# One ring of small buffers for residual rows and weight sums, the second SwiGLU product opened inside the first, and the residual added late

## The chip, the cores and the metric

The kernel runs on one core of a Trainium2 chip. The time is the device time of one execution in microseconds (us), lower is better; the figure of a kernel is the median of its timed runs. Every array is float32.

## The reference, cut to what matters

One layer of an encoder with 1024 frames (S) of 1024 channels (D): a mixer of two recurrent branches with a residual, then a SwiGLU with a residual, then a last RMS norm. The mixer is untouched here. The SwiGLU has 2816 hidden channels.

```python
def swiglu(xn, w_ffn_in, w_ffn_out):
    gate, up = _split(xn @ w_ffn_in, (D_FF, D_FF))
    return (jax.nn.silu(gate) * up) @ w_ffn_out
...
        h = h + hybrid_mixer(rms_norm(h, norm1_g[l]), ...)
        h = h + swiglu(rms_norm(h, norm2_g[l]), w_ffn_in[l], w_ffn_out[l])
    return rms_norm(h, norm_f)
```

## The kernel before

**Precision.** A float32 operand is kept as a high part (rounded to the matmul's type) and a low part. `split` makes them: ScalarE casts the high part (L84), VectorE subtracts it from the source (L85). A product is then three matmuls: high by high, high by low, low by high.

**Loads.** `add` puts a load into a plan, `load_next` issues the next one (L96, on SP's queue), `split_next` splits the oldest loaded tile and issues the next load. The raw tiles are two buffers, `w_raw`, used in turn (`act_raw` uses the same two).

**Order.** Each engine runs its own instructions in a fixed order, which the tile scheduler writes when the program is built; an instruction that waits holds up all that stand behind it on its engine. A tile named with a `tag` and `bufs` is one of a ring of so many buffers; the next user of a buffer waits for the last reader of the former. Pools that are opened after others are closed lie on the same memory and wait in the same manner.

**p5: the mixer's last projection and the second norm.** `hres[c]`, eight tiles of 128 rows (chunks c = 0 to 7), hold the residual. For each chunk `out_proj` (L147 with `mm`) adds the projection to it, `norm2_rows` norms it into `xr` and stores the row to `h_dram`, and `norm2_turn` transposes it on TensorE (L201), copies the result on ScalarE to `xb` (L858) and forms the differences of Winograd's form of Strassen's product on VectorE and GpSimd (L862 to L865). From these `block` splits seven operands of 4 x 512 columns: `b11`, `b21`, `t1`, `t2`, `b22`, `t3`, `t4`. The second half (`t1` to `t4`, `b22`) needs chunk 7.

**ffn_in: the first product.** A unit u (22 of them) is 128 gate and 128 up channels. It is seven products p of 12 matmuls of 128x128 by 128x512 (`product`, L809), in the order of the list `seq`; the weight of product (u, p) is a block of the raw weight or one of four sums (`unit_sums`, four GpSimd instructions L797 to L800, into `s1` to `s4`), split into a tile `wc` (`weight`; three buffers are in the pool `wearly`, five in the pool of ffn_in). After some products `after` evacuates the PSUM bank: `e1` (L934), `sg` (silu, L937), `u2`, `e5`, `u3` and so on; after product 4 the activation row `act` is stored to `act_dram` (L956). Weights are prepared four products ahead (`LEAD`). Units 0 and 1 begin inside p5, with products (0,1) and (1,1); their evacuations and sums come after p5.

**ffn_out: the second product.** The 22 chunks of hidden channels are cut into pieces of (4, 4, 4, 4, 4, 2). For each piece its weights and activation rows are loaded and split into `slot` tiles; then for each chunk c of rows and each half of columns `mm_tok` does 3 matmuls for each hidden chunk (L147 with `aux`), and VectorE adds the bank to `hres[c]` (L1046), which was loaded again from `h_dram` (L1027, tiles `hr`). In the last piece ScalarE squares and sums the row (L1048) into `o`, of two buffers `o7`; VectorE forms the factor and the output (L1061, for the last half row ScalarE at L1059), and two stores of a half row each go out (L1063).

Of the kernel before, what the change touches and what calls it, by code (L numbers as in the profile page):

```python
# [9 lines left out]
F32 = mybir.dt.float32  # L10
# [3 lines left out]
ALU = mybir.AluOpType  # L14
# [18 lines left out]
def hybrid_block_kernel(  # L33
# [780 lines left out]
    hres = [h_pool.tile([P, D], F32, name=f"h{c}") for c in range(NC)]  # L814
# [4 lines left out]
    def weight(u, p, pool=None):  # L819
# [4 lines left out]
        wready[u, p] = t  # L824

    with phase("p5", "right") as pp:
# [66 lines left out]
        for c in range(4, NC):  # L893
# [8 lines left out]
            if c == 6:  # L902
                unit_load(1)
                weight_a = {1: raws[0][0][:, 0:4], 2: raws[0][0][:, 4:8]}
                sums[0] = weight_a
                weight(0, 1)
                weight(0, 2)
        turn_late()
        sums[1] = {1: raws[1][0][:, 0:4]}
        weight(1, 1)  # L910
        banks = {}
# [4 lines left out]
        for name, src, i, j in (("t1", xb[0][0], 0, 0), ("t2", t2, 0, 0), ("b22", xb[1][1], 1, 1),  # L916
                                ("t3", xb[1][0], 1, 1), ("t4", xb[0][1], 0, 1)):
            block(name, src, i, j)
    h_stack.close()


    with phase("ffn_in", "right") as pp:
        def tmp(tag, bufs):
            t = pp.tile([P, 512], F32, name=tag, tag=tag, bufs=bufs)
            return t

        part = {}

        def after(u, p):
            b1, b2, b3 = banks[u, 1], banks.get((u, 6)), banks.get((u, 5))  # L930
            d = part.setdefault(u, {})
            if p == 1:
                d["e1"] = tmp("e1", 2)
                nc.scalar.copy(out=d["e1"], in_=b1)  # L934
            elif p == 2:
                d["sg"] = tmp("sg", 2)
                nc.scalar.activation(out=d["sg"], in_=b1, func=AF.Silu)  # L937
            elif p == 6:
                d["u2"] = tmp("u2", 2)
                nc.vector.tensor_tensor(out=d["u2"], in0=b2, in1=d["e1"], op=ALU.add)  # L940
            elif p == 5:
# [25 lines left out]
        def prepare(i):  # L967
            if i >= len(seq) or seq[i] in wready:
                return
# [126 lines left out]
```

## Time and profile before

| | us |
|---|---|
| median of three timed runs | 2128.44 (2128.12 to 2130.18) |
| the profiled execution's own time | 2135.46 |
| its span | 2133.8 |
| TensorE busy in the span | 2032.1 |
| VectorE, ScalarE, GpSimd busy | 1234.2, 839.4, 446.3 |

The profiled execution is one execution with the profiler on, and it took 7.0 us longer than the median. Its span runs from the first to the last recorded instruction. The first SwiGLU product lies between 1408 and 1852 us of the span, the second between 1852 and the end. The mean granted clock of TensorE is 0.981 of full speed.

### The profile page before, as it was taken

The page shows a single profiled execution, that of the slowest core. Times are in us where ns is not written, and L with a number is a line of the kernel's source. Part 1 is how long each engine was busy: PE and PEld are TensorE (multiplying, and loading weights), DVE is VectorE, ACT ScalarE, POOL GpSimd, SP SyncE. Part 2 cuts the span into 40 slices and gives each one's busy share as a digit, 9 for nine tenths or more (in the row PEclk, how much of TensorE's full clock was granted, in tenths as well). Part 3 has the DMA queues.
Part 4 walks back from the last instruction along what each step waited for, and adds up shares of the span by engine and source line. Part 5 has one row for each costly group of instructions (what it writes and reads, how often), then busy time and mean ns, then how long its engine had stood idle before and what let it go on. Part 6 is the DMA issues. An engine that isn't in the chain of part 4 may idle for free.

```text
span 2133.8 us, 23957 instructions
## 1 busy us (share of the span) xinstructions
PE 2032.1 (95%) x9206; PEld 1659.8 (78%) x9206; DVE 1234.2 (58%) x2178; ACT 839.4 (39%) x1156; POOL 446.3 (21%) x318
## 2 busy tenths in 40 slices
PE   6999999999999998999999999979999999789996
PEld 4778888777787786788888888858888888678885
DVE  6677667778768779634431215567455555344436
ACT  5886744544544544421131113443333333222202
POOL 3100004324324325200100110025333333000000
PEclk9999999999999999999999999989999999999998
DMA  3222231322321321322141114322222223343302
GB/s 131 62 70 61 81 104 41 95 87 65 89 76 59 114 75 50 109 89 89 50 128 50 50 50 162 105 77 76 85 79 90 88 63 96 137 150 117 108 33 79
DMA packets 178806, 182.28 MB, mean 85 GB/s; under 512 B 9404, under 2 KB 145028, under 8 KB 178692
## 3 DMA queue, kind: packets, MB, share of 16 engines
q1 hardware_dynamic: 178692, 180.76, 27.0%
q8 instruction: 72, 1.18, 0.2%
q14 instruction: 42, 0.34, 0.1%
HBM read 148.10 MB, written 32.64 MB: 85 GB/s over the span
## 4 chain that ended last, share of the span: by engine, by line
PE 76%; DVE 12%; DMA 6%; issue 3%; ACT 2%; POOL 0%; SPq 0%; DVEq 0%; ACTq 0%; POOLq 0%
PE mm L136 34%; PE mm L809 19%; PE aux L147 11%; PE mm L147 8%; DVE ed L546 2%; DMA ed<-acs_dram 2%; DMA w_raw<-in_w_in_dram 2%; PE aux L592 1%; DVE rs_t L158 1%; DVE ed L574 1%; DMA act_raw<-act_dram 1%; PE aux L425 1%; DVE w_lo L85 1%; DMA y_dram<-xd 1%; DVE rs_r L160 1%
## 5 line engine op out<-in xcount | busy, mean ns | idle before, releaser
L809 PE MATMUL mm<-slot,wc 128*128 128x512 f32 x1848 | 426.9, 393 | 14.5 <-ACT e L934 13.9
L809 PEld LDWEIGHTS mm<-slot,wc 128*128 128x128 f32 x1848 | 348.6, 189 | 91.4 <-ACT e L934 14.2
L136 PE MATMUL mm<-xn_lo,w_hi 128*128 128x512 f32 x896 | 355.0, 396 | 0.6 <-DVE xn_lo L206 0.6
L136 PE MATMUL mm<-xn_hi,w_hi 128*128 128x512 f32 x896 | 355.2, 397 | 0.0
L136 PE MATMUL mm<-xn_hi,w_lo 128*128 128x512 f32 x896 | 354.4, 396 | 0.0
L147 PE MATMUL aux<-slot,slot 128*128 128x512 f32 (+1 forms) x1062 | 246.9, 395 | 16.5 <-ACT slot L84 11.2
L147 PEld LDWEIGHTS aux<-slot,slot 128*128 128x128 f32 x1062 | 202.1, 191 | 61.4 <-ACT slot L84 12.5
L136 PEld LDWEIGHTS mm<-xn_lo,w_hi 128*128 128x128 f32 x896 | 170.5, 190 | 37.9 <-DVE xn_lo L206 1.1
L136 PEld LDWEIGHTS mm<-xn_hi,w_lo 128*128 128x128 f32 x896 | 170.4, 190 | 37.3
L136 PEld LDWEIGHTS mm<-xn_hi,w_hi 128*128 128x128 f32 x896 | 170.1, 190 | 36.5
L85 DVE TENSOR_TENSOR w_lo<-w_raw,w_hi 128x1024 fp32r<-128x1024 f32 x80 | 106.7, 1334 | 139.1 <-ACT w_hi L84 139.0
L147 PE MATMUL mm<-wz,xn_hi 128*128 128x512 f32 x512 | 161.3, 395 | 0.0
L84 ACT CAST w_hi<-w_raw 128x1024 fp32r<-128x1024 f32 x80 | 83.6, 1045 | 178.1 <-PE mm L136 157.4
L1046 DVE TENSOR_TENSOR hr<-aux,hr 128x512 f32<-128x512 f32 (+1 forms) x97 | 65.3, 683 | 97.8 <-PE aux L147 97.7
L147 PEld LDWEIGHTS mm<-wz,xn_hi 128*128 128x128 f32 x512 | 94.5, 188 | 18.5
L147 PE MATMUL mm<-wz,xn_lo 128*128 128x512 f32 x256 | 101.1, 395 | 0.0
L84 ACT CAST slot<-w_raw 128x1024 fp32r<-128x1024 f32 x34 | 35.5, 1051 | 166.2 <-PE aux L147 80.3
L84 ACT CAST wc<-s 128x512 fp32r<-128x512 f32 x88 | 54.4, 620 | 113.1 <-PE mm L809 108.5
L85 DVE TENSOR_TENSOR wc<-s,wc 128x512 fp32r<-128x512 f32 x88 | 74.2, 845 | 36.2 <-ACT wc L84 34.9
L546 DVE TENSOR_SCALAR ed<-ed,acs_t 128x128 f32<-128x128 f32 x256 | 80.8, 381 | 22.5 <-DMA ed<-acs_dram 22.3
L147 PE MATMUL mm<-slot,slot 128*128 128x512 f32 x384 | 89.2, 391 | 0.0
L136 PE MATMUL mm<-v_even,w_hi 128*128 128x512 f32 x256 | 84.7, 405 | 0.0
(270 smaller groups left out, 3231.1 us busy)
## 6 DMA issues: line engine op xcount, KB each, us to landing
w_raw<-in_w_in_dram SPq DMA_DIRECT2D x72, 512.0 KB, 3.9
ed<-acs_dram SPq DMA_DIRECT2D x32, 512.0 KB, 4.3
w_raw<-in_w_branch_dram SPq DMA_DIRECT2D x24, 512.0 KB, 3.4
w_raw<-in_w_ffn_in_dram SPq DMA_DIRECT2D x22, 512.0 KB, 3.9
raw_pair<-in_w_ffn_in_dram SPq DMA_DIRECT2D x22, 512.0 KB, 5.3
act_dram<-act SPq DMA_DIRECT2D x22, 512.0 KB, 2.9
w_raw<-in_w_ffn_out_dram SPq DMA_DIRECT2D x22, 512.0 KB, 3.6
act_raw<-act_dram SPq DMA_DIRECT2D x22, 512.0 KB, 3.9
```

The costliest lines, as they stand in the source:

```text
L84: nc.scalar.copy(out=hi, in_=src)
L85: nc.vector.tensor_tensor(out=lo, in0=src, in1=f32(hi), op=ALU.subtract)
L136: nc.tensor.matmul(ps[:m, :], ww[:, k, :], xx(p, k, h), start=(k == 0 and i == 0), stop=(k == nk - 1 and i == 2))
L147: nc.tensor.matmul(ps, xx(p, k), ww(q, k), start=(k == 0 and i == 0), stop=(k == nk - 1 and i == 2))
L158: nc.vector.tensor_tensor(out=t, in0=r, in1=r, op=ALU.mult)
L160: nc.vector.scalar_tensor_tensor(out=r, in0=t, scalar=1.5, in1=r, op0=ALU.add, op1=ALU.mult)
L425: nc.tensor.matmul(pg, w[:, j, :], uu[:, hs], start=(q == 0), stop=(q == 2))
L546: nc.vector.tensor_scalar(out=ed[:, h, :], in0=ed[:, h, :], scalar1=acs_t[:, c, h0 + h:h0 + h + 1], scalar2=0.0, op0=ALU.subtract, op1=ALU ...
L574: nc.vector.tensor_tensor(out=ed, in0=ed, in1=sc.unsqueeze(1).broadcast_to([P, HG, P]), op=ALU.mult)
L592: nc.tensor.matmul(pd[:, h * 64:(h + 1) * 64], ed[:, h, :], xdt[:, h, :], start=True, stop=True)
L809: nc.tensor.matmul(ps, w[:, p, k, :], x[q][:, k, :], start=(start and k == 0 and i == 0), stop=(k == 3 and i == 2), skip_group_check=True)
L1046: nc.vector.tensor_tensor(out=hres[c][:, ns], in0=po, in1=hres[c][:, ns], op=ALU.add)
```

## The change

Four things change.

A ring `hbuf` of eight buffers of 128x1024 float32 holds the residual rows of p5, and after them the sums of a unit (in two pairs, `s12` and `s34`), `e1` with `sg`, `u2` with `u3`, and `e5`. It stays open until the end of ffn_in.

The sums of units 0 and 1 are made inside p5, at chunks 5 and 6. Their products (0,1), (1,1) and now also (0,2) are issued there with their evacuations.

The second product's plan is made before ffn_in, with pieces of (2, 4, 4, 4, 4, 4). In the last unit, 21, two loads are issued after product 6 and one item is split after each of the products 5, 2, 7 and 3: the whole first piece.

The rows are no longer loaded ahead of the second product. ScalarE copies the first piece's result into `hres[c]` (L1056 after), and in the third piece (`f0 == 6`) the row is loaded from `h_dram` into `hl` (L1049) and added by GpSimd (L1050). The PSUM banks of the second product come in turn from the rings `aux` (three) and `mm` (four).

```diff
+    def hbuf(name, shape):
+        t = h_pool.tile(shape, F32, name=name, tag="hbuf", bufs=8)
+        return t
+
+    hres = [hbuf(f"h{c}", [P, D]) for c in range(NC)]
...
-    def unit_sums(u, pool):
+    def unit_sums(u):
...
-        s1, s2, s3, s4 = (pool.tile([P, 4, P], F32, name=f"s{i}", tag="wsum", bufs=4) for i in range(1, 5))
+        (s1, s2), (s3, s4) = ([t[:, 0], t[:, 1]] for t in (hbuf("s12", [P, 2, 4, P]), hbuf("s34", [P, 2, 4, P])))
...
+    def pair(u, name):
+        t = hbuf(name, [P, 2, 512])
+        return t[:, 0], t[:, 1]
...
         if p == 1:
-            d["e1"] = tmp("e1", 2)
+            d["e1"], d["sg"] = pair(u, "e1_sg")
...
-            if c == 6:
+            if c == 5:
                 unit_load(1)
+                unit_sums(0)
                 weight(0, 1)
                 weight(0, 2)
+            if c == 6:
+                unit_sums(1)
+                weight(1, 1)
         turn_late()
-        for u, p in ((0, 1), (1, 1)):
-            banks[u, 1] = bank("mm")
-            product(banks[u, 1], wready.pop((u, p)), xc[XOF[p]], True)
+        opened(0, 1)
+        opened(1, 1)
         turn_late()
+        block("t1", xb[0][0], 0, 0)
+        opened(0, 2)
+        block("t2", t2, 0, 0)
...
-        seq = [(0, 2), (0, 5), (0, 6), (0, 3), (0, 7), (1, 6), (0, 4), (1, 5), (1, 2), (1, 7), (1, 3), (2, 1), (1, 4)]
+        seq = [(1, 2), (0, 5), (0, 6), (0, 3), (0, 7), (1, 6), (0, 4), (1, 5), (1, 7), (1, 3), (2, 1), (1, 4)]
...
+            opened(u, p)
+            if u == NFT - 1:
+                if p == 6:
+                    load_next()
+                    load_next()
+                elif p in (5, 2, 7, 3):
+                    split_next()
...
-        for nk in (4, 4, 4, 4, 4, 2):
+    for nk in (2, 4, 4, 4, 4, 4):
...
-        for c in range(NC):
-            nc.sync.dma_start(out=hres[c], in_=h_dram[c * P:(c + 1) * P, :])
...
+                if f0 == 6:
+                    hl = pp.tile([P, D], F32, name="hl", tag="hl", bufs=2)
+                    nc.sync.dma_start(out=hl, in_=h_dram[c * P:(c + 1) * P, :])
+                    nc.gpsimd.tensor_tensor(out=hres[c], in0=hres[c], in1=hl, op=ALU.add)
...
-                    po = bank()[:, :b - a]
+                    po = bank("mm" if c % 2 else "aux")[:, :b - a]
...
+                    if not f0:
+                        nc.scalar.copy(out=hres[c][:, ns], in_=po)
+                        continue
```

The diff says little of the order on the engines, so three places are shown. The first is TensorE's order where row chunk 7 is transposed (`xr_10479` before, `xr_10494` after, is chunk 7's normed row; `slot_10316` and `slot_10317` are `b11`, `slot_10363` and `slot_10364` are `b21`, `slot_10571` and `slot_10572` are `t1`). Before:

```order
L809 MATMUL mm<-slot_10317,wc 128x512
L809 MATMUL mm<-slot_10316,wc 128x512
L201 MATMUL aux<-ident,xr_10479 128x128 x8
L809 MATMUL mm<-slot_10363,wc 128x512
L809 MATMUL mm<-slot_10364,wc 128x512
```

After:

```order
L809 MATMUL mm<-slot_10363,wc 128x512 x2
L809 MATMUL mm<-slot_10364,wc 128x512
L809 MATMUL mm<-slot_10363,wc 128x512
L201 MATMUL aux<-ident,xr_10494 128x128 x8
L809 MATMUL mm<-slot_10363,wc 128x512
L809 MATMUL mm<-slot_10364,wc 128x512
L809 MATMUL mm<-slot_10571,wc 128x512
L809 MATMUL mm<-slot_10572,wc 128x512
```

Before, the transposes stand right behind product (1,1) and ahead of (0,2); after, they stand behind (0,2), and (1,2) is the first product behind them, woven with the first two matmuls of (0,5).

The second place is ScalarE's order there, from chunk 6's last copies to the casts of the last blocks. Before:

```order
L858 COPY xb_10395<-aux 128x4x128
L84 CAST wc<-w_raw 128x512
L858 COPY xb_10396<-aux 128x4x128
L858 COPY xb_10395<-aux 128x4x128
L858 COPY xb_10396<-aux 128x4x128
L84 CAST slot_10567<-xb_10396 128x1024 x2
L84 CAST slot_10555<-xb_10041 128x1024 x2
L84 CAST slot_10573<-xb_10395 128x1024 x2
L84 CAST slot_10561<-t_9799 128x1024 x2
L934 COPY e_10590<-mm 128x512
L934 COPY e_10592<-mm 128x512
L84 CAST wc<-s_10594 128x512
```

After (`s_10443` is a sum of unit 1):

```order
L905 COPY xb_10410<-aux 128x4x128
L842 COPY e_sg<-mm 128x512
L905 COPY xb_10411<-aux 128x4x128
L84 CAST wc<-s_10443 128x512
L842 COPY e_sg<-mm 128x512
L84 CAST wc<-w_raw 128x512
L844 ACT_TABLE_LOAD
L844 ACTIVATE e_sg<-mm 128x512
L84 CAST wc<-s_10443 128x512
L905 COPY xb_10410<-aux 128x4x128
L905 COPY xb_10411<-aux 128x4x128
L84 CAST slot_10596<-xb_10411 128x1024 x2
L84 CAST slot_10571<-xb_10041 128x1024 x2
```

The first evacuations, two casts of unit 1's sums and the silu with its table load have moved ahead of chunk 7's copies (the last two `xb` rows), and the `e1` copies no longer stand behind the casts of `t`.

The third place is SP's queue of DMA issues around the last unit. Before:

```order
L956 DMA act_dram<-act 128x1024 x2
L96 DMA w_raw<-in_w_ffn_out_dram 128x2x512
L96 DMA act_raw<-act_dram 128x1024
L956 DMA act_dram<-act 128x1024
L1027 DMA hr_13577<-h_dram 128x1024
L1027 DMA hr_13578<-h_dram 128x1024
L1027 DMA hr_13579<-h_dram 128x1024
L96 DMA w_raw<-in_w_ffn_out_dram 128x2x512
L1027 DMA hr_13580<-h_dram 128x1024
L96 DMA act_raw<-act_dram 128x1024
L1027 DMA hr_13581<-h_dram 128x1024
L1027 DMA hr_13582<-h_dram 128x1024
```

After:

```order
L96 DMA act_raw<-act_dram 128x1024
L96 DMA w_raw<-in_w_ffn_out_dram 128x2x512
L862 DMA act_dram<-act 128x1024 x2
L96 DMA act_raw<-act_dram 128x1024
L96 DMA w_raw<-in_w_ffn_out_dram 128x2x512
L96 DMA act_raw<-act_dram 128x1024
L96 DMA w_raw<-in_w_ffn_out_dram 128x2x512
L1036 DMA g_bc_13526<-in_norm_f_dram 128x1024
L1049 DMA hl<-h_dram 128x1024 x2
L96 DMA act_raw<-act_dram 128x1024
L862 DMA act_dram<-act 128x1024
L96 DMA w_raw<-in_w_ffn_out_dram 128x2x512
```

Before, the loads of the rows `hr` stand between the first loads of the second product. After, those eight are gone from there; the first item's loads stand ahead of two stores of `act`, and the store of unit 21's `act` stands behind three more activation rows, two weights, `g_bc` and two loads of `hl`.

## Rows read from the trace of the kernel before

**Rows 1.** The page's chain that ended last: share of the span by engine.

```profile
PE 76%; DVE 12%; DMA 6%; issue 3%; ACT 2%; POOL 0%; SPq 0%; DVEq 0%; ACTq 0%; POOLq 0%
```

**Rows 2.** The page's groups: name and shapes xcount | busy, mean ns | idle before, releaser.

```profile
L809 PE MATMUL mm<-slot,wc 128*128 128x512 f32 x1848 | 426.9, 393 | 14.5 <-ACT e L934 13.9
...
L147 PE MATMUL aux<-slot,slot 128*128 128x512 f32 (+1 forms) x1062 | 246.9, 395 | 16.5 <-ACT slot L84 11.2
...
L1046 DVE TENSOR_TENSOR hr<-aux,hr 128x512 f32<-128x512 f32 (+1 forms) x97 | 65.3, 683 | 97.8 <-PE aux L147 97.7
```

**Rows 3.** Table of stretches: length, busy time of each engine, PEclk, DMA share, GB/s.

```profile
1420.00:1436.00 16.00, 4.66 (x11) 3.71 (x12) 13.41 (x11) 8.08 (x11) 6.76 (x5) 0.50 0.00 0
1550.00:1840.00 290.00, 290.00 (x1269) 237.95 (x1268) 148.38 (x195) 96.54 (x164) 99.22 (x71) 1.00 0.25 80
1858.00:1870.00 12.00, 5.58 (x13) 4.10 (x14) 2.45 (x2) 2.09 (x2) 0.00 (x0) 0.50 1.01 400
1890.00:2080.00 190.00, 190.00 (x840) 157.34 (x839) 86.26 (x103) 33.26 (x32) 0.00 (x0) 1.00 0.28 89
```

**Rows 4.** Timeline of TensorE, gap 1: start, length, line, tiles [idle before <-releaser].

```profile
1416.33 1.06 PE L201 MATMUL aux<-ident,xr 128*128 128x128 f32 x8 [1.18 <-DVE xr L847]
1431.34 11.98 PE L809 MATMUL mm<-slot,wc 128*128 128x512 f32 x40 [13.95 <-ACT e L934]
1443.85 6.46 PE L809 MATMUL mm<-slot,wc 128*128 128x512 f32 x27 [0.53 <-DVE wc L85]
```

**Rows 5.** Timeline of VectorE, gap 1.

```profile
1410.26 0.69 DVE L862 TENSOR_TENSOR xb<-xb,xb 128x512 f32<-128x512 f32 x1
...
1417.61 1.45 DVE L862 TENSOR_TENSOR xb<-xb,xb 128x512 f32<-128x512 f32 x1 [0.23 <-ACT xb L858]
...
1420.37 7.97 DVE L85 TENSOR_TENSOR slot<-xb,slot 128x1024 fp32r<-128x1024 f32 x6
1428.26 2.34 DVE L85 TENSOR_TENSOR slot<-t,slot 128x1024 fp32r<-128x1024 f32 x2
```

**Rows 6.** Timeline of ScalarE and GpSimd, gap 1.

```profile
1416.86 1.65 POOL L865 TENSOR_TENSOR xb<-xb,t 128x512 f32<-128x512 f32 x1 [3.36 <-DVE t L863]
...
1430.70 1.07 ACT L934 COPY e<-mm 128x512 f32<-128x512 f32 x2 [4.93 <-DVE slot L85]
1430.74 1.29 POOL L797 TENSOR_TENSOR s<-w_raw 128x512 f32<-128x512 f32 x1 [9.16 <-issue]
...
1438.01 1.28 ACT L937 ACT_TABLE_LOAD   x1
```

**Rows 7.** Timeline of TensorE, gap 2.

```profile
1852.31 0.63 PE L147 MATMUL aux<-slot,slot 128*128 128x512 f32 x2
...
1864.42 7.91 PE L147 MATMUL aux<-slot,slot 128*128 128x512 f32 x21 [8.81 <-ACT slot L84]
...
1875.99 4.13 PE L147 MATMUL aux<-slot,slot 128*128 128x512 f32 x11 [0.76 <-DVE slot L85]
1882.49 77.88 PE L147 MATMUL aux<-slot,slot 128*128 128x512 f32 x335 [2.37 <-DVE hr L1046]
```

**Rows 8.** Timeline of ScalarE, gap 2.

```profile
1863.32 1.04 ACT L84 CAST slot<-w_raw 128x1024 fp32r<-128x1024 f32 x1 [10.32 <-DMA w_raw<-in_w_ffn_out_dram]
...
1885.58 1.04 ACT L84 CAST slot<-w_raw 128x1024 fp32r<-128x1024 f32 x1 [2.76 <-DMA w_raw<-in_w_ffn_out_dram]
...
1898.19 1.05 ACT L84 CAST slot<-w_raw 128x1024 fp32r<-128x1024 f32 x1 [1.64 <-DMA w_raw<-in_w_ffn_out_dram]
```

**Rows 9.** DMA issues from 1835 to 1900: xcount, KB each, median us to landing.

```profile
hr<-h_dram SPq DMA_DIRECT2D x8, 512.0 KB, 9.1
w_raw<-in_w_ffn_out_dram SPq DMA_DIRECT2D x7, 512.0 KB, 3.7
```

**Rows 10.** Timeline of the last 74 us: TensorE's last row, ScalarE's last square.

```profile
2059.71 56.01 PE L147 MATMUL aux<-slot,slot 128*128 128x512 f32 x252
...
2126.58 0.40 ACT L1048 ACTIVATE o<-hr 128x256 f32<-128x256 f32 x1
```

More of the change, by code (lines that the diff above doesn't have):

```diff
@@ L912, in hybrid_block_kernel @@
[L912 to L914 removed]
+        opened(0, 1)
+        opened(1, 1)
         turn_late()
[L916 to L917 removed]
+        block("t1", xb[0][0], 0, 0)
+        opened(0, 2)
+        block("t2", t2, 0, 0)
+        for name, src, i, j in (("b22", xb[1][1], 1, 1), ("t3", xb[1][0], 1, 1), ("t4", xb[0][1], 0, 1)):
@@ new lines, in hybrid_block_kernel, with add_act, then, act_raw @@
+    acts, pieces, f0 = {}, [], 0
+    def add_act(f):
+        def then(raw):
+            acts[f] = slot(1)
+            split(acts[f][:, 0, :], acts[f][:, 1, :], raw)
+        def act_raw():
+            t = stream.tile([P, S], F32, name="act_raw", tag="w_raw", bufs=2)
+            return t
+        add(act_dram[f * P:(f + 1) * P, :], then, act_raw)
+    def add_wf(n, q, f0, wf):
+        def then(raw):
+            if q == 0:
+                wf[n] += [quad(slot(0)), quad(slot(0))]
+            split(wf[n][0][:, 2 * q:2 * q + 2, :], wf[n][1][:, 2 * q:2 * q + 2, :], raw)
+        add(w_cols(w_ffn_out, n * 512, 512, (f0 + 2 * q) * P, 2), then)
@@ L961, in hybrid_block_kernel @@
+    for nk in (2, 4, 4, 4, 4, 4):
+        wf = [[], []]
+        pieces.append((f0, nk, wf))
+        for n in range(2):
+            for q in range(nk // 2):
+                add_act(f0 + n * (nk // 2) + q)
+                add_wf(n, q, f0, wf)
+        f0 += nk
+    with phase("ffn_in", "right") as pp:
+        seq = [(1, 2), (0, 5), (0, 6), (0, 3), (0, 7), (1, 6), (0, 4), (1, 5), (1, 7), (1, 3), (2, 1), (1, 4)]
         for u in range(2, NFT):
@@ L964, in hybrid_block_kernel @@
         left[0], left[1] = 5, 6
-        whole = set()
+        whole = {0, 1}
         def prepare(i):
-            if i >= len(seq) or seq[i] in wready:
+            if i >= len(seq):
                 return
@@ L971, in prepare @@
             if u not in whole:
-                unit_sums(u, pp)
+                unit_sums(u)
                 whole.add(u)
@@ L977, in prepare @@
                 unit_load(u + 2)
-        after(0, 1)
-        after(1, 1)
         LEAD = 4
-        for i in range(1, LEAD):
+        for i in range(LEAD):
             prepare(i)
@@ L985, in hybrid_block_kernel @@
             prepare(i + LEAD)
-            if HOME[p] == p:
-                banks[u, p] = bank("mm")
-            product(banks[u, HOME[p]], wready.pop((u, p)), xc[XOF[p]], HOME[p] == p)
-            after(u, p)
+            opened(u, p)
[5 more added lines that the diff above has]
+                    split_next()
+    h_stack.close()
     h_pool = ctx.enter_context(phase("h_pool2", "right"))
@@ L1031, in hybrid_block_kernel @@
         for f0, nk, wf in pieces:
-            order = [f0 + 2 * q + n for n in range(2) for q in range(nk // 2)]
-            ts = dict(zip(order, acts[f0:f0 + nk]))
             last = f0 + nk == NFT
```

99 lines of the change are left out of this document (33 added, 66 removed).

## The prediction, made before the changed kernel was run

> **What bounds the kernel now.** The page's chain [rows 1] comes first: TensorE is 76% of the chain that ended last. So the kernel is bound by its matmuls, and a change can win only where TensorE stands still, runs at its lower clock, or has finished. The page's groups [rows 2] then say where it stands still in the SwiGLU: 14.5 us ahead of the first product's matmuls (L809), 13.9 of it for ScalarE's `e`, and 16.5 us ahead of the second's (L147 with `aux`), 11.2 of it for ScalarE's splits. The table of stretches [rows 3] says what lies between: from 1550 to 1840 TensorE is busy for 290.00 of 290 us at clock 1.00, from 1890 to 2080 for 190.00 of 190 with 840 matmuls (0.226 us each). After 2116 it has no more to do [rows 10]. Three places are left: gap 1 near 1420, gap 2 near 1855, and the tail. Both gaps cost twice: the clock is 0.50 (1.2 of 2.4 GHz) from 1420 to 1436 and again from 1858 to 1870, each time after TensorE had stood still.
>
> **Gap 1.** Before the gap TensorE has done 24 of the first-product matmuls; it ends with the eight transposes of row chunk 7 [rows 4]. It restarts at 1431.34, does 40 matmuls in 11.98 us and waits 0.53 us for a weight, so matmul 65 starts at 1443.85. The chain through the gap is in [rows 5]: once ScalarE has copied the transposes, VectorE forms the Winograd differences (from 1417.61) and then subtracts eight low parts, 7.97 us and 2.34 us, the last two reading `t2` and ending at 1430.60. `e` may be copied only then, since its buffer lies where `t2` did; the copy starts at 1430.70 [rows 6].
> The change gives `e1` a buffer of the shared ring, so that wait goes. But the weight tiles `wc` of the ffn_in pool now lie where `t2` lay: the first of them, for product (1,2), waits for the same last subtraction, and TensorE's next matmul needs it. I therefore move the wait and don't remove it. What is gained: product (0,2) is now issued ahead of the transposes, so 36 matmuls and not 24 are done before the gap (12 x 0.229 = 2.75 us; 0.229 is 290 us by the 1269 matmuls of [rows 3]), and the 0.53 us wait for a sum goes, since the sums of units 0 and 1 are already made. What is lost: the transposes of chunk 7 stand behind those 12 matmuls. Before, TensorE waited 1.18 us for them [rows 4], so they slip by 2.75 - 1.18 = 1.57 us, and ScalarE has an `e1` copy, two casts, the table load (1.28 us [rows 6]) and a silu ahead of its own copies; I take 2.3 us for the whole slip. Net: 2.75 + 0.53 - 2.3 = **1.0 us gained**. If the slip is only 1.57 us it is 1.7; if it is 5 us, with the three weight subtractions that now precede chunk 7 on VectorE, it is -1.7.
> The slip has a second source. VectorE's first difference took 0.69 us for chunk 5, with GpSimd idle, and 1.45 us for chunk 7 [rows 5], with a GpSimd subtraction running since 1416.86 [rows 6]. The change puts unit 1's four sums (1.29 us each, as at 1430.74 [rows 6]) beside the norms of chunks 6 and 7, and chunk 7's transposes wait for its norm. I let each second sum hold up one VectorE instruction, 2 x 0.76 = 1.5 us, about half of it felt behind the 12 matmuls: hence 2.3 and not 1.57. The Trainium skill ("SBUF — State Buffer", Who interferes with whom) states that a VectorE instruction with two SBUF inputs contends with a GpSimd instruction that reads SBUF. If by that rule all four sums held one up, the slip would be about 3.1 us and the term 0.2. The row of 1.45 us agrees with the rule; how often it strikes no row tells.
>
> **Gap 2.** TensorE's stretch from 1852.31 to the end of its last matmul at 2115.73 [rows 7, 10] is 263.4 us for 1062 matmuls, which are 1056 of full width. Without a stop, 1056 x 0.226 = 239 us. So 24.4 us are to be had: the 16.5 us of waits and the rest at half clock (21 matmuls in 7.91 us instead of 4.75, 11 in 4.13 instead of 2.49). The cause is in [rows 8]: ScalarE waits 10.3 us for weights of the second product, because eight 512 KB rows `hr` are issued between the weight loads; their median time to landing is 9.1 us against 3.7 us for a weight [rows 9].
> The change removes those eight loads from here, makes the first piece two chunks deep instead of four, and loads and splits its four items during unit 21, behind steady matmuls. The splits there cost 1.04 us on ScalarE [rows 8] and 1.2 us on VectorE each (two in 2.34 us [rows 5]); in the steady part ScalarE is busy for 96.5 and VectorE for 148.4 of 290 us [rows 3], so they are hidden. In TensorE's order six and then eleven matmuls of the second product stand among the last products of unit 21; they need `act` chunks 0 and 1, written long ago, and weights asked for some 10 us ahead, so I expect no wait there. Piece 1 is 2 x 3 x 16 = 96 matmuls, 21.7 us. In it the loads for piece 2 must come: eight items of 512 KB through two buffers. One cycle (load 3.7, cast 1.04, subtraction 1.2, two buffers in turn) ran at one item per 3.2 us (ScalarE's casts at 1885.58 and 1898.19 are four items apart [rows 8]). The first goes out some 2 us before unit 21 ends, so at 3.2 us each the seventh is split 20 us after that end and the eighth by 25; by TensorE's order they are first needed 24.3 and 27.7 us after it. The margin is 3 to 4 us, which is thin, and the store of `act` 21, `g_bc` and two rows of `hl` stand in SP's queue among these loads. I take 1 us of stall: **gap 2 gives 23.4 us**. If each load is 1 us slower, the stall is 3 to 5 us; if two of them are held as the `hr` rows held them, 10 us.
> New work: 16 copies of 128x512 on ScalarE in place of 16 VectorE adds (about 0.55 us each, as the `e` copies: 1.07 us for two [rows 6]), and eight GpSimd adds of 128x1024 with their loads in the third piece. A GpSimd subtraction of 128x512 took 1.65 us beside VectorE [rows 6], so an add of double the size 3.3 us, 26 us in all, in a piece of 43.4 us where GpSimd has nothing else. VectorE's add of the same chunk waits for it, with the later chunks' adds queued behind; with three and four PSUM banks in turn TensorE runs five half rows, 13.6 us, ahead before it stops. Cost taken: nothing; uncovered, one add, 3.3 us.
>
> **Tail.** TensorE ends at 2115.73 and the span at 2133.8: 18.07 us [rows 10]. The last piece is two chunks deep, so a row chunk takes TensorE 2.7 us, while the norm of a row takes longer: ScalarE's squares wait for the store of the row two earlier since `o7` has two buffers. So the norms run behind and finish alone. With four chunks in the last piece a row takes 5.43 us, and the norms keep up. Then only the last row's own chain is left. Its last square starts about 0.7 us after the last matmul (an add of a quarter row, which I put at 0.45 us from the 0.68 us of L1046's half rows [rows 2], and the hand-overs), and from there to the end took 2133.8 - 2126.58 = 7.2 us. I take 8.1 us with a little queueing: **10.0 us gained**, 9 at the least, 11 at the most.
>
> **The rest of ffn_in.** The ring of eight 4 KB buffers is asked for five times a unit where separate buffers stood before. On average fewer than five are live, and each buffer's former user ends several products earlier, so I cost it at nothing; the cover is one unit's 84 matmuls, 19.2 us.
>
> **Sum.** 1.0 + 23.4 + 10.0 = 34.4 us. The profiled execution took 2135.5 us, so its like would take 2101.1. It was 7.0 us above the median of the timed runs, and the same saving from 2128.44 gives **2094 us**.
>
> **Rivals.**
> A. Piece 2's weights come late. For it: [rows 8, 9], loads were late here before, and the margin is 3 to 4 us. Against it: the eight row loads are gone. It gives back 5 to 10 us, half clock included: 2099 to 2104.
> B. Gap 1 grows, by the contention of [rows 5, 6] or by the longer queues on ScalarE and VectorE ahead of chunk 7: 3 to 5 us lost and not 1 gained, 2098 to 2100. In the same class: a tail that saves only half, 2099.
> C. The other side: the shared ring makes TensorE wait in every unit. The decision is the buffer of `e1` and `sg`: asked for at product 1 of the next unit, it is the one that, eight requests back, held a sum or `u2`/`u3`. If TensorE lost 1.7 us in each of 20 units, that is 34 us and the gain is gone; at 2 us, 2134. For it: rings tie unrelated users together. Against it: TensorE is busy for 290.00 of 290 us and by the program's order each buffer's last reader stands several products ahead of its next writer.
> D. That the change doesn't do what it says in gap 1, where a wait on `t2` stays, is in the forecast already. The rival is that it does: with weights ready early TensorE would not stand still after the transposes, gap 1 would give up to 14 us and the time be 2081. Against it stands the order of the buffers.
>
> **How the numbers follow.** Forecast (2089 to 2098) 0.60; A 0.17; B 0.12; C 0.04; D 0.04; something that costs the last unit dearly without ending slower, 0.03. The range from 2088 to 2105 takes in the forecast, B and most of A. About 0.2% (4.3 us) is what a measurement of this kernel can tell from no change. Only C comes near it: faster 0.95, same 0.02, slower 0.03.
>
> **What would show it.** In the profile after: TensorE's longest wait still near 14 us in gap 1, now for a `wc` cast, with matmul 65 at 1442 to 1444; no wait over 1 us between 1840 and 1880, and the clock at 1.00 there; L1056 on ScalarE in place of the adds; GpSimd's adds in the third piece about 3.3 us each; TensorE's end some 8 us before the span's. Wrong if TensorE waits for `wc` or for `e1_sg` inside the units, if it waits for `slot` in piece 2 by more than 5 us, or if ScalarE still waits for output stores.

## The result, and the profile after

The changed kernel takes 2096.47 us (2095.67 to 2098.21, four runs) against 2128.28 us of the kernel before in the same comparison (2127.82 to 2130.18): 31.8 us less, ratio 0.985, 95% interval 0.9833 to 0.9867. The forecast was 2094 us, with 2088 to 2105 as its range.

Executions of one and the same kernel differ by several us for reasons that lie outside the change: the mixer ahead of the SwiGLU ends earlier or later, and in some executions each matmul of the first product takes 0.233 us instead of 0.229 throughout (shown at the end). So each profile is read from a start of its own, the first matmul of the first product (L809). In the profile of before it came at 1408.49, in that of after at 1401.31. These 7.2 us are not the change's: 7.1 of them have arisen by the 3500th of the 6280 TensorE instructions ahead of that matmul, some 790 us into the span, where the two kernels are the same.

```profile
1408.49 2.55 PE L809 MATMUL mm<-slot,wc 128*128 128x512 f32 x10
```

From that start the kernels compare as follows. "Matmul 100" is the start of the hundredth L809 matmul, found by counting in the timeline of TensorE; six other profiles with the same gap 1 gave 44.4 to 45.4 us, so a value within that band says nothing.

| us from the start | before | after | difference |
|---|---|---|---|
| chunk 7's transposes | 7.8 | 11.7 | +3.9 |
| restart in gap 1 | 22.85 | 28.64 | +5.8 |
| matmul 100 | 43.5 | 44.9 | +1.4 |
| TensorE's end | 707.2 | 684.9 | -22.4 |
| end of the span | 725.3 | 692.8 | -32.4 |

The terms follow: gap 1 lost 1.4 us (0.9 to 1.9 by the band), the stretch from matmul 100 to TensorE's end (gap 2) gained 22.4 + 1.4, which is 23.7 before rounding, and the tail went from 18.0 to 7.9, 10.1 gained. Together 32.4 us of the traces, against 31.8 by the medians.

The page of after answers to [rows 1, 2]; first the chain, then groups (idle before and its releaser at the end):

```profile
PE 78%; DVE 12%; DMA 5%; issue 2%; ACT 1%; SPq 1%; POOL 0%; DVEq 0%; ACTq 0%; POOLq 0%
...
L809 PE MATMUL mm<-slot,wc 128*128 128x512 f32 x1848 | 426.3, 393 | 16.6 <-ACT wc L84 15.8
...
L147 PE MATMUL mm<-slot,slot 128*128 128x512 f32 (+1 forms) x924 | 213.9, 387 | 0.0
...
L147 PE MATMUL aux<-slot,slot 128*128 128x512 f32 x528 | 124.4, 389 | 0.0
```

The second product no longer waits at all. The first still does, for a `wc` cast now and 15.8 us instead of 13.9. The stretches (length, busy time of PE, PEld, DVE, ACT, POOL, PEclk, DMA share, GB/s) answer to [rows 3]: no pause and full clock from the steady part through gap 2's place to the end.

```profile
1550.00:1840.00 290.00, 290.00 (x1269) 237.93 (x1268) 158.18 (x194) 95.54 (x165) 114.72 (x71) 1.00 0.26 82
1840.00:1856.00 16.00, 16.00 (x72) 13.19 (x71) 8.09 (x9) 7.43 (x12) 1.29 (x1) 1.00 0.74 254
1856.00:1880.00 24.00, 24.00 (x107) 19.87 (x106) 10.19 (x9) 13.46 (x18) 0.00 (x0) 1.00 0.53 166
```

Gap 1 in TensorE's timeline, which answers to [rows 4]:

```profile
1401.31 2.55 PE L809 MATMUL mm<-slot,wc 128*128 128x512 f32 x10
...
1408.67 3.02 PE L809 MATMUL mm<-slot,wc 128*128 128x512 f32 x12 [0.71 <-ACT e_sg L842]
1413.01 1.09 PE L201 MATMUL aux<-ident,xr 128*128 128x128 f32 x8 [1.32 <-DVE xr L894]
1429.95 40.41 PE L809 MATMUL mm<-slot,wc 128*128 128x512 f32 x168 [15.85 <-ACT wc L84]
```

Behind the restart the clock comes back sooner than before. These are the first 6 us behind it in before (first row) and in after (second row); the first busy time is TensorE's, and the clock is the third figure from the end:

```profile
1431.34:1437.34 6.00, 6.00 (x15) 4.77 (x16) 2.80 (x2) 2.16 (x4) 5.92 (x5) 0.54 0.15 42
```

```profile
1429.95:1435.95 6.00, 6.00 (x19) 4.82 (x20) 4.18 (x5) 2.83 (x6) 3.42 (x3) 0.70 0.00 0
```

The 12 matmuls of (0,2) stand ahead of the transposes, as forecast, and even so the transposes wait 1.32 us for chunk 7's normed row. VectorE says why; this answers to [rows 5]:

```profile
1403.98 1.65 DVE L910 TENSOR_TENSOR t<-xb,xb 128x512 f32<-128x512 f32 x1
1405.56 1.79 DVE L911 TENSOR_TENSOR xb<-xb,xb 128x512 f32<-128x512 f32 x1
...
1408.55 1.22 DVE L159 SCALAR_TENSOR_TENSOR rs_t<-rs_t,rs_v 128x1 f32<-128x1 f32 x1
...
1410.30 1.26 DVE L160 SCALAR_TENSOR_TENSOR rs_r<-rs_t,rs_r 128x1 f32<-128x1 f32 x1
...
1414.07 1.76 DVE L85 TENSOR_TENSOR wc<-s,wc 128x512 fp32r<-128x512 f32 x1
1415.76 0.68 DVE L85 TENSOR_TENSOR wc<-w_raw,wc 128x512 fp32r<-128x512 f32 x1
1416.36 0.68 DVE L85 TENSOR_TENSOR wc<-s,wc 128x512 fp32r<-128x512 f32 x1
1416.96 0.68 DVE L909 TENSOR_TENSOR xb<-xb,xb 128x512 f32<-128x512 f32 x1
...
1418.95 7.97 DVE L85 TENSOR_TENSOR slot<-xb,slot 128x1024 fp32r<-128x1024 f32 x6
1426.84 2.35 DVE L85 TENSOR_TENSOR slot<-t,slot 128x1024 fp32r<-128x1024 f32 x2
```

Four instructions ahead of chunk 7's row are stretched from 0.69 and 0.16 us to 1.22 to 1.79. GpSimd runs beside each of them, without a pause from 1403.77 to 1411.53:

```profile
1403.77 1.31 POOL L797 TENSOR_TENSOR s<-raw_pair 128x512 f32<-128x512 f32 x1 [5.08 <-DMA raw_pair<-in_w_ffn_in_dram]
1405.05 1.76 POOL L799 TENSOR_TENSOR s<-raw_pair 128x512 f32<-128x512 f32 x1
1406.77 1.73 POOL L798 TENSOR_TENSOR s<-s,raw_pair 128x512 f32<-128x512 f32 x1
1408.46 1.29 POOL L912 TENSOR_TENSOR xb<-xb,t 128x512 f32<-128x512 f32 x1
1409.71 1.82 POOL L800 TENSOR_TENSOR s<-raw_pair,s 128x512 f32<-128x512 f32 x1
```

The two short ones (L159, L160) end at 1409.77 and 1411.56, 0.02 and 0.03 us behind the GpSimd instruction beside them. L912 is no sum but a difference of chunk 6 that the sums have pushed back.

Then three weight subtractions, 3.1 us, stand between the transposes and chunk 7's first difference at 1416.96. ScalarE's queue, which is longer now, costs nothing there: it waits 0.66 us for the transposes before it copies them, and the copies end at 1414.77.

```profile
1413.70 1.07 ACT L905 COPY xb<-aux 128x512 f32<-128x512 f32 x2 [0.66 <-PE aux L201]
```

The block subtractions behind take as long as before, 7.97 and 2.35 us. VectorE's load between the start and `t2`'s last low part, in before (first row) and in after (second), each from its own table:

```profile
1408.49:1430.60 22.11, 7.72 (x43) 6.05 (x41) 20.28 (x26) 13.07 (x19) 4.97 (x3) 0.76 0.13 42
```

```profile
1401.31:1429.19 27.88, 10.77 (x55) 8.22 (x53) 26.05 (x28) 17.04 (x25) 11.06 (x7) 0.77 0.17 52
```

VectorE (the third busy time) is busy for 20.28 of 22.11 us, then for 26.05 of 27.88: its own 5.77 us more are the restart's 5.8. The four stretches (4.2 us) and the three subtractions (3.1) are more than that, since before the change a weight subtraction (0.69 us) and the stretch of the 1.45 us difference [rows 5] stood in the same place.

The end of TensorE's timeline, beside a span of 2094.1 us, answers to [rows 10]; the two GpSimd rows are the first three adds of the residual (seven of the eight took 2.4 us, one 3.3):

```profile
2080.43 5.75 PE L147 MATMUL mm<-slot,slot 128*128 128x512 f32 x36
```

```profile
1880.95 2.41 POOL L1050 TENSOR_TENSOR hr<-hr,hl 128x1024 f32<-128x1024 f32 x1 [36.24 <-DVE hr L1058]
1885.13 5.67 POOL L1050 TENSOR_TENSOR hr<-hr,hl 128x1024 f32<-128x1024 f32 x2 [1.76 <-DVE hr L1058]
```

Before, ScalarE's squares waited six times for the store of an earlier row in the last 49 us (us in total, times, longest); after, no square waits for a store.

```profile
ACT o L1048 <- DMA out_dram<-o: 7.9, 6, 1.9
```

### The profile page after: what moved, and what is told of

Same layout as the page of the kernel before. It is cut to its first block, busy times and chain, and to the rows that moved or that the text cites. A ratio compares the mean times of both kernels' runs of the same rounds, so it can differ in the third digit from the quotient of the medians.

```text
span 2094.1 us, 23931 instructions
## 1 busy us (share of the span) xinstructions
PE 2017.3 (96%) x9212; PEld 1651.0 (79%) x9212; DVE 1238.3 (59%) x2162; ACT 844.8 (40%) x1172; POOL 484.5 (23%) x326
## 4 chain that ended last, share of the span: by engine, by line
PE 78%; DVE 12%; DMA 5%; issue 2%; ACT 1%; SPq 1%; POOL 0%; DVEq 0%; ACTq 0%; POOLq 0%
PE mm L136 34%; PE mm L809 20%; PE mm L147 14%; PE aux L147 6%; DVE ed L546 2%; DMA w_raw<-in_w_in_dram 2%; DMA ed<-acs_dram 2%; DVE rs_t L158 1%; DVE ed L574 1%; PE aux L592 1%; DMA y_dram<-xd 1%; DVE w_lo L85 1%; PE aux L425 1%; DVE xd L617 1%; PE turn L516 1%
## 5 line engine op out<-in xcount | busy, mean ns | idle before, releaser
L809 PE MATMUL mm<-slot,wc 128*128 128x512 f32 x1848 | 426.3, 393 | 16.6 <-ACT wc L84 15.8
L809 PEld LDWEIGHTS mm<-slot,wc 128*128 128x128 f32 x1848 | 347.9, 189 | 93.2 <-ACT wc L84 16.1
L147 PE MATMUL mm<-slot,slot 128*128 128x512 f32 (+1 forms) x924 | 213.9, 387 | 0.0
L147 PEld LDWEIGHTS mm<-slot,slot 128*128 128x128 f32 x924 | 171.5, 188 | 34.9
L85 DVE TENSOR_TENSOR w_lo<-w_raw,w_hi 128x1024 fp32r<-128x1024 f32 x80 | 106.7, 1333 | 138.8 <-ACT w_hi L84 138.7
L147 PE MATMUL aux<-slot,slot 128*128 128x512 f32 x528 | 124.4, 389 | 0.0
L147 PEld LDWEIGHTS aux<-slot,slot 128*128 128x128 f32 x528 | 99.1, 188 | 20.6
L85 DVE TENSOR_TENSOR wc<-s,wc 128x512 fp32r<-128x512 f32 x88 | 62.8, 731 | 55.5 <-ACT wc L84 55.0
L858 POOL TENSOR_TENSOR u_u<-u_u,e 128x512 f32<-128x512 f32 x22 | 37.5, 1703 | 244.0 <-DVE u_u L852 231.2
L568 POOL TENSOR_TENSOR xwf<-xdt,dte_t 128x512 f32<-128x512 f32 x28 | 30.5, 1090 | 229.7 <-DVE xdt L564 229.2
```

What stands on the lines that cost most here:

```text
L85: nc.vector.tensor_tensor(out=lo, in0=src, in1=f32(hi), op=ALU.subtract)
L147: nc.tensor.matmul(ps, xx(p, k), ww(q, k), start=(k == 0 and i == 0), stop=(k == nk - 1 and i == 2))
L568: nc.gpsimd.tensor_tensor(out=xwf, in0=xdt, in1=bcast(dte_t[:, c, hs], 64), op=ALU.mult)
L809: nc.tensor.matmul(ps, w[:, p, k, :], x[q][:, k, :], start=(start and k == 0 and i == 0), stop=(k == 3 and i == 2), skip_group_check=True)
L858: nc.gpsimd.tensor_tensor(out=d["u3"], in0=d["u3"], in1=d["e5"], op=ALU.add)
```

## The experiments

All edits are against the changed kernel. Where a median and the reading from the start disagree, the reading decides, for the reason given above; both are told. The kernel before was timed again beside each group of experiments and took 2126.6 to 2127.2 us there, 1.1 to 1.7 less than beside the changed kernel; differences between the medians of an experiment and of the changed kernel carry that too.

### Gap 1: what sets the restart

**A wc that doesn't touch t2.** 

```diff
         for i in range(LEAD):
             prepare(i)
+        pad = pp.tile([P, 96], F32, name="pad")
+        nc.vector.memset(pad, 0.0)
```

> Only change against the changed kernel: one extra tile of 384 bytes in the ffn_in pool, behind the wc ring, so that the first wc of that pool, of product (1,2), no longer lies on the first 384 bytes of t2 but on g_bc alone. Theory 'memory': the overlap with t2 sets when TensorE restarts in gap 1, so TensorE goes on behind the transposes with the 12 matmuls of (1,2), the long wait shrinks from 15.8 us to some 12 and the time falls by 3 to 5 us, to 2092 to 2093. Theory 'order': the subtraction of that wc stands on VectorE behind all subtractions of the second half's operands anyway, so only ScalarE's cast goes earlier, TensorE still restarts after the last subtraction of t2, and at most 0.7 us is gained: 2096 and not distinguishable.

```profile
1421.46 2.08 PE L809 MATMUL mm<-slot,wc 128*128 128x512 f32 x4 [9.92 <-ACT wc L84]
1427.35 33.05 PE L809 MATMUL mm<-slot,wc 128*128 128x512 f32 x135 [3.81 <-DVE wc L85]
```

These are its restart rows; its start is at 1399.07. ScalarE's cast came early and let four matmuls through at half clock, then TensorE waited for the subtraction (`DVE wc L85`) until 28.3 us after the start, as in the changed kernel (28.6). Matmul 100 came at 43.5 instead of 44.9. So the memory under `wc` is not what sets the restart; VectorE's order is. The median, 2098.7 us (2097.56 to 2100.5), is higher; the profiled execution is one of those with slower matmuls, which cost it some 6 us. The other three have no trace.

**Unit 1's sums later.** 

```diff
             if c == 6:
-                unit_sums(1)
+                sums[1] = {1: raws[1][0][:, 0:4]}
                 weight(1, 1)
...
-        whole = {0, 1}
+        whole = {0}
```

> Undoes one part: unit 1's four GpSimd sums are no longer asked for at chunk 6 but with the other units' sums, after p5. Theory 'contention': these sums run beside chunk 7's norm on VectorE and stretch it (four instructions took 1.06 to 1.79 us instead of 0.16 to 0.69), so without them chunk 7's transposes start 2 to 3 us earlier against the first product, gap 1's slip falls from 5.8 to 3 us and the time to 2093.5 to 2095. Theory 'queue': the slip comes from the three weight subtractions (3.1 us) that stand ahead of chunk 7's differences on VectorE; they are still made before t2's low part, so the slip stays near 5.8 us, less 0 to 1, and the time 2096. If the sums now meet the block subtractions, up to 3 us is lost again.

Median 2095.65 us. TensorE's rows and then VectorE's, chunk 7's differences (start at 1401.00):

```profile
1410.37 1.09 PE L201 MATMUL aux<-ident,xr 128*128 128x128 f32 x8
1429.27 31.00 PE L809 MATMUL mm<-slot,wc 128*128 128x512 f32 x126 [17.81 <-ACT wc L84]
```

```profile
1411.68 1.51 DVE L909 TENSOR_TENSOR xb<-xb,xb 128x512 f32<-128x512 f32 x1 [0.16 <-ACT xb L905]
1413.29 1.58 DVE L910 TENSOR_TENSOR t<-xb,xb 128x512 f32<-128x512 f32 x1
1414.79 1.75 DVE L911 TENSOR_TENSOR xb<-xb,xb 128x512 f32<-128x512 f32 x1
```

The transposes come 2.3 us earlier (9.4 instead of 11.7 us after the start), as the theory "contention" had it. But two of the four sums, and a difference on GpSimd, now run beside chunk 7's differences on VectorE and stretch those, and the weight subtractions have only moved behind four of the block subtractions. The restart stays at 28.3. Both theories are half right: each names work that VectorE has to do before `t2`, and moving it within that stretch gains nothing.

**(1,2)'s weight early, alone and with the later sums.** 

```diff
-        early = slots_used[0] % 8 < 3
+        early = slots_used[0] == 3 or slots_used[0] % 8 < 3
```

> Only change: the wc of product (1,2) takes a buffer of wearly, which is free long before, and so is split ahead of chunk 7's norm; the weights of the next products move one buffer on. Theory 'order': TensorE now has 12 matmuls to do right behind the transposes, 2.75 us, and the later restart stays at t2's last subtraction; 2.5 to 3 us less work after the gap: 2093 to 2094. Theory 'queue': one more weight subtraction ahead of chunk 7's differences makes everything 0.7 to 1.5 us later, so the gain is 1 to 2 us: 2095. If the restart doesn't depend on (1,2)'s weight at all, no gain.

> Both of the last two edits: (1,2)'s weight in wearly, and unit 1's sums asked for after p5. If contention and the late weight are separate costs, the gains add: 2.7 us for the 12 matmuls and 2 to 3 us for the shorter norm of chunk 7, 2090.5 to 2092. If the contention only moves (the sums then meet the block subtractions), it is no better than g_early12 alone.

Medians 2092.59 us (2092.07 to 2099.7) and 2093.23 us (2090.8 to 2100.82). The restart of the first, whose start is at 1399.69:

```profile
1428.77 21.58 PE L809 MATMUL mm<-slot,wc 128*128 128x512 f32 x81 [13.73 <-ACT wc L84]
```

In both TensorE does the 12 matmuls right behind the transposes; the restart is at 29.1 and 28.9 us, 0.4 and 0.3 us later, and matmul 100 at 43.6 and 42.8. That is 1.2 and 2.1 us gained, less than the 2.75 of the 12 matmuls: VectorE has one subtraction more ahead of `t2`. The gains don't add to the 5 us that separate costs would have given.

**Less work for VectorE.** The low part of `b22` is left out of the computation and copied by ScalarE.

```diff
+                if name == "b22":
+                    nc.scalar.copy(out=xc[name][0][:, ks], in_=src[:, ks])
+                    nc.scalar.copy(out=xc[name][1][:, ks], in_=src[:, ks])
+                else:
+                    split(xc[name][0][:, ks], xc[name][1][:, ks], src[:, ks])
```

> Leaves out a part of the computation: the low part of the operand b22 is not subtracted but copied from the source by ScalarE, so VectorE has two subtractions of 128x1024 less ahead of t2's low part (2.35 us). Theory: VectorE, busy without a pause from the first product's start to t2's last subtraction, is what sets the restart in gap 1, so TensorE restarts 2.3 us earlier, 26 and not 28.4 us after its first first-product matmul, and the time falls by as much: about 2094. Rival: the restart is set by something else in the chain (ScalarE's casts, the transposes), and ScalarE's two more casts make it later: 28.5 us or more, 2096 to 2098.

```profile
1428.16 22.14 PE L809 MATMUL mm<-slot,wc 128*128 128x512 f32 x84 [13.58 <-ACT wc L84]
```

The start is at 1402.07, so the restart came 26.1 us after it, 2.2 to 2.5 earlier than in the kernels with the same order (28.3 to 28.6), and the median is 2092.94 us (2090.62 to 2095.44). So much VectorE work less, so much earlier the restart: VectorE is the bound of gap 1. Not all of it arrives: matmul 100 and the end of the span come 1.6 us earlier than in the changed kernel.

### Gap 2: prefetch, rows, sizes

**No prefetch.** 

```diff
-            if u == NFT - 1:
-                if p == 6:
-                    load_next()
-                    load_next()
-                elif p in (5, 2, 7, 3):
-                    split_next()
+    for _ in range(4):
+        split_next()
     h_stack.close()
```

> Undoes one part: the first piece is no longer loaded and split during unit 21; the four items are split after ffn_in (the scheduler still puts the first two loads and one cast ahead). Theory: gap 2's 23.7 us come from the prefetch, the smaller first piece and the missing row loads together; without the prefetch alone TensorE waits for the second activation row and the second weight, one item per 3.2 us and 6 us for the first, so 4 to 9 us with its half clock come back: 2100 to 2106. Rival: the missing row loads alone closed gap 2 and the prefetch buys nothing: 2096 to 2098.

Median 2102.10 us (2101.62 to 2102.85), 5.6 more. Its waits of TensorE (us in total, times, longest):

```profile
PE aux L147 <- ACT slot L84: 3.0, 1, 3.0
PE aux L147 <- DVE slot L85: 1.7, 1, 1.7
```

4.7 us of waits, and the clock stayed at 1.00 from 1855 on.

**The rows loaded ahead, as before.** 

```diff
+        for c in range(NC):
+            nc.sync.dma_start(out=hres[c], in_=h_dram[c * P:(c + 1) * P, :])
         g_bc = pp.tile([P, D], F32, name="g_bc7")
...
-                if f0 == 6:
-                    hl = pp.tile([P, D], F32, name="hl", tag="hl", bufs=2)
-                    nc.sync.dma_start(out=hl, in_=h_dram[c * P:(c + 1) * P, :])
-                    nc.gpsimd.tensor_tensor(out=hres[c], in0=hres[c], in1=hl, op=ALU.add)
...
-                    if not f0:
-                        nc.scalar.copy(out=hres[c][:, ns], in_=po)
-                        continue
```

> Undoes one part: the eight residual rows are loaded again ahead of the second product and VectorE adds the first piece to them, as before the change; the prefetch, the piece sizes and the banks stay. Theory: the eight row loads, 4 MB at some 400 GB/s, stand in SP's queue ahead of the loads for the second piece and push them back by some 10 us, of which the margin of the first piece absorbs 3 to 4 and the rest is stall and half clock: 6 to 10 us lost, 2102 to 2107. Rival: with the first piece already split the row loads are hidden, no more than 2 us are lost: under 2099.

Median 2103.77 us (2099.15 to 2106.5), 7.3 more. From the end of the first product to TensorE's end it takes 241.8 us, the changed kernel 235.7: 6.1 us are due to this place, with two waits and a clock of 0.83 from 1875 to 1885:

```profile
PE aux L147 <- ACT slot L84: 2.5, 1, 2.5
PE aux L147 <- DVE hr L1053: 1.4, 1, 1.4
```

The row loads are not hidden behind a prefetched piece.

**A first piece of four.** The pieces are (4, 2, 4, 4, 4, 4), and after ffn_in four more items are split.

```diff
-    for nk in (2, 4, 4, 4, 4, 4):
+    for nk in (4, 2, 4, 4, 4, 4):
...
+    for _ in range(4):
+        split_next()
     h_stack.close()
```

> Changes one size: pieces of (4, 2, 4, 4, 4, 4), so that the four prefetched items are half of the first piece and the other four are split after unit 21. Theory: the small first piece matters as much as the prefetch; TensorE waits for the fifth to seventh item at 3.2 us each: 4 to 9 us lost with the half clock, 2101 to 2106. Rival: the longer first piece gives its own items time, and nothing is lost: 2095 to 2098.

Median 2093.98 us (2093.35 to 2102.93), and not one wait of TensorE behind the first product. My theory is wrong here. The scheduler wove the rows: from 1856 to 1871 TensorE's timeline has groups of 1 to 10 matmuls that alternate between `aux` and `mm`, so it seems to take the first two hidden chunks of one row after the other, each in a bank of its own, while the other items arrive. Half a piece split ahead is enough; the size of the first piece is not what closed gap 2.

**The residual one piece earlier.** 

```diff
-                if f0 == 6:
+                if f0 == 2:
```

> Moves one part: the residual rows are loaded and added in the second piece, not the third. Theory: the second piece's loads have a margin of 3 to 4 us and eight 512 KB row loads among the third piece's loads are absorbed, since a piece of 43.4 us has room for sixteen items at 3.2 us only just; 0 to 4 us lost, 2096.5 to 2100. Rival: the place of the residual is free, no change; or it is decisive: SP's queue is held by a row load that waits for its buffer, and 6 us or more are lost.

Median 2101.56 us (2093.64 to 2104.42), too wide to read. By its profile (2093.64 us) TensorE has no wait in the second product and ends 685.2 us after the start, against 684.9. In that execution the place is free. It is the fastest of the four; the others took 2100.25 to 2104.42 us and have no trace, so whether the place costs something in them is not shown.

### Tail and ring

**A last piece of two.** 

```diff
-    for nk in (2, 4, 4, 4, 4, 4):
+    for nk in (2, 4, 4, 4, 4, 2, 2):
```

> Undoes one part: the pieces are (2, 4, 4, 4, 4, 2, 2), so the last piece is again two chunks deep. Theory: the tail's 10.2 us come from the length of a row in the last piece alone, so TensorE ends where it did and the span some 18 us later instead of 7.9: 2106 to 2107. Rival: part of the tail's gain is that the rows' first adds moved elsewhere, and less than 7 us come back: under 2103.

Median 2104.30 us (2103.4 to 2105.65), 7.8 more. Its last row of TensorE, beside a span of 2102.2 us:

```profile
2082.25 2.04 PE L147 MATMUL mm<-slot,slot 128*128 128x512 f32 x14
```

TensorE ends 684.4 us after the start, as in the changed kernel, and the tail is 17.9 us, as before the change (18.0): 10.0 us of the tail come back with the length of the last piece alone.

**Seven requests to the ring.** 

```diff
-            d["e1"], d["sg"] = pair(u, "e1_sg")
+            d["e1"], _ = pair(u, "e1")
...
+            d["sg"], _ = pair(u, "sg")
...
-            d["u2"], d["u3"] = pair(u, "u2_u3")
+            d["u2"], _ = pair(u, "u2")
...
+            d["u3"], _ = pair(u, "u3")
```

> Doubles a suspected cost: e1 and sg, and u2 and u3, each take a buffer of their own from the ring, so that a unit asks for seven and not five of the eight. If the ring is near its limit (rival C of the prediction), each buffer comes free later than it is asked for and TensorE waits in every unit: 1 us or more in each of 20 units, over 2116. If the ring has the slack that the forecast gave it, the reuse distance falls from 1.6 to 1.14 units and evacuations or sums begin to wait without TensorE standing still: 2096 to 2100.

Median 2094.59 us (2092.11 to 2102.41). In the steady part TensorE has no pause (PE is the first busy time):

```profile
1500.00:1800.00 300.00, 300.00 (x1313) 246.13 (x1312) 164.47 (x204) 97.80 (x172) 121.27 (x77) 1.00 0.27 85
```

Even at seven of eight buffers a unit the ring costs nothing.

### A faster version

```diff
-        early = slots_used[0] % 8 < 3
+        early = slots_used[0] < 5 or slots_used[0] % 8 < 3
...
         opened(1, 1)
+        weight(1, 2)
         turn_late()
+        weight(0, 5)
...
-        left[0], left[1] = 5, 6
+        left[0], left[1] = 4, 5
...
-            if i >= len(seq):
+            if i >= len(seq) or seq[i] in wready:
```

> A version meant to beat the changed kernel: the weights of (1,2) and (0,5) take buffers of wearly and are asked for inside p5, so TensorE can do (1,2) behind the transposes and (0,5) as soon as t1 is split, ahead of t2. Theory: the restart on t2 stays near 28.5 to 29 us after the first product's start, but 24 matmuls (5.5 us) less are left behind it, less 0.7 us for the weight that now stands ahead of chunk 7: 4 us less than the changed kernel, 2092 to 2093; with one matmul stretch in the middle of the gap at half clock perhaps 1 us of it is lost. Rival: VectorE's extra work ahead of t2 eats it: 2095 to 2097.

Median 2089.49 us (2089.06 to 2091.4), ratio to before 0.983 (0.9815 to 0.9844), 7.0 us under the changed kernel. TensorE's gap is now three short ones (start at 1402.09):

```profile
1414.46 3.01 PE L809 MATMUL mm<-slot,wc 128*128 128x512 f32 x12
1419.41 0.50 PE L809 MATMUL mm<-slot,wc 128*128 128x512 f32 x1 [1.94 <-ACT slot L84]
1424.22 4.36 PE L809 MATMUL mm<-slot,wc 128*128 128x512 f32 x11 [4.30 <-DVE slot L85]
1431.20 19.16 PE L809 MATMUL mm<-slot,wc 128*128 128x512 f32 x76 [2.62 <-ACT wc L84]
```

Product (1,2) runs behind the transposes and (0,5) as soon as `t1` is split. Matmul 100 comes at 39.6 us, 5.2 earlier, about the 24 matmuls (5.5 us) that no longer stand behind the restart at 29.1. By the trace it is 5.2 us to the end of the span too. Of the other 1.8 of the medians, 1.7 are those by which the kernel before was faster in this comparison (2126.58 against 2128.28 us).

## Why the prediction came out right

**Gap 1: the wait as forecast, its size off, its cause given only in part, and the sign of the term wrong.** The wait moved from `e` to `wc` and 36 matmuls were done before it, as forecast; it took 15.85 us where "near 14" was written. The step that was mis-sized is the slip, "I take 2.3 us for the whole slip": it is 5.8 us. Two parts of it were in the text with too small a price. I let "each second sum hold up one VectorE instruction"; the trace has four stretched, by 0.96, 1.10, 1.06 and 1.10 us, as many as in the prediction's other count and at a higher price than the 0.76 us of the row. The Trainium skill ("SBUF — State Buffer", Who interferes with whom) states that a VectorE instruction with two SBUF inputs contends with a GpSimd instruction that reads SBUF; the trace agrees in all four. And the three weight subtractions ahead of chunk 7 were kept as a bound ("if it is 5 us, ... it is -1.7") where they belonged in the sum: they stood in the program's order, behind chunk 7's transposes on an engine that is busy for 26.05 of 27.88 us there. The longer queue on ScalarE, which the prediction names beside them, cost nothing.

The measured term is -1.4 and not +1.0. Of the 5.8 us, 2.75 and 0.53 came back as forecast, and some 1.2 more because less was lost at half clock behind the restart (40 matmuls in 11.98 us before, 2.8 more than at 0.229; 64 in 16.2 us after, 1.6 more). That last part stood in no sum, so it was luck that the term was not worse.

The cause that the prediction gave for the wait, the memory of `wc` on that of `t2`, is not what bounds it: without that overlap four matmuls pass early, and TensorE still restarts for good at 28.3 us. VectorE is full from the start to `t2`, so the restart follows its sum of work, and neither the place of the sums nor the memory of `wc` changes it by more than 0.4 us. What it would bring to take the sums or the three subtractions out of that stretch altogether was not run.

**Gap 2: right.** Forecast 23.4 us with 1 us of stall, measured 23.7 with none; TensorE has no wait in the second product, so the loads came in time. Undone one at a time, the prefetch is worth 5.4 us (from the end of the first product, the matmuls that it had taken in counted) and the removed row loads 6.1; neither brings back the other 12 us. How these divide, with both undone at once, and what the seven banks in place of three do, was not run. The smaller first piece, which I described as a part of the remedy, is not needed. The GpSimd adds took 2.4 us and not 3.3, but for one, and hid. The expectation for the residual one piece earlier also has a wrong sum: sixteen items at 3.2 us are 51 us, more than the 43.4 us of a piece.

**Tail: right.** Forecast 10.0, measured 10.1, and 10.0 by undoing it alone. The squares no longer wait for stores, as the mechanism had it. The step "8.1 us with a little queueing" is 7.9, in part by luck: the last square starts 1.5 us after the last matmul and not 0.7, and from there to the end it takes 6.5 us and not 7.2.

**The rest of ffn_in: right.** TensorE is busy for 290.00 of 290 us with 1269 matmuls, the same counts as in [rows 3]; rival C had no ground even with seven requests a unit.

**The sum.** 34.4 us forecast, 32.4 by the traces: gap 1's term is 2.4 short, gap 2 0.3 and the tail 0.1 over. The medians have 31.8, and so 2096.5 stands against 2094. That the profiled execution of before was 7.0 us longer than the median fits its late start of the first product, 7.2 us against after, and subtracting the gain from the median was right. Rival B is what happened, at less than half its price (1.4 us lost, not 3 to 5); A and C did not; D's direction is what the faster version takes a third of.

## What to carry to other kernels

At a restart that waits for one engine, add up that engine's work from the last common point and treat everything that the order puts ahead of the awaited instruction as path, however small; here, moving a piece within that stretch gained 0.4 us at most, and taking 2.35 us out brought the restart 2.2 to 2.5 us forward. Give the stalled engine work that depends on less: two early weights brought more than every repair of the wait itself. And read a change of a few us from a point near it in the trace, since the medians here spread by as much.

## What the runs showed of the hardware that was not expected

In some executions each matmul of the first product takes 1.5 to 2% longer over the whole product, at a granted clock of 1.00. The same stretch in the changed kernel (first row) and in the one with the padded pool (second row); the columns are the length, PE, PEld, PEclk, DMA share and GB/s:

```profile
1500.00:1800.00 300.00, 300.00 (x1312) 246.15 (x1311) 1.00 0.27 83
```

```profile
1500.00:1800.00 300.00, 300.00 (x1292) 242.33 (x1291) 1.00 0.26 83
```

1312 and 1292 matmuls in 300 us, 0.2287 and 0.2322 us each, some 6 us over the product's 1748 matmuls behind the hundredth. It was seen in four of the fourteen profiles; the second product's cadence, 0.227 us, was the same in all. The kernel with a first piece of four has it in its profile (2102.93 us) and, to judge by their times alone (2093.4 to 2094.1), not in its other runs, so the code does not seem to be the cause. What it is stays open.

The length of a pause does not alone say whether the clock falls behind it: without the prefetch TensorE waited 1.7 and 3.0 us and the clock was 1.00 in every stretch read after it; with the rows loaded ahead it waited 1.4 and 2.5 us and 9 matmuls behind the second pause took 3.64 us, at a mean clock of 0.83 from 1875 to 1885. In the first kernel (first row) the stretch begins just ahead of the end of the second pause, in the other (second row) it holds the second pause; the clock is the third figure from the end:

```profile
1855.00:1865.00 10.00, 9.39 (x41) 7.81 (x42) 4.21 (x4) 6.80 (x11) 0.00 (x0) 1.00 0.43 129
```

```profile
1875.00:1885.00 10.00, 7.50 (x26) 5.71 (x25) 5.15 (x5) 2.21 (x3) 0.00 (x0) 0.83 0.42 140
```
